# MLP up projection: high and low part of the left operand in one moving operand of 512 columns, and one weight sum formed by an accumulating load

## The chip, the cores and the metric

The kernel runs on one core of one Trainium2 chip. The metric is device time in microseconds of one execution. Lower is better. Before the change the median of three runs is 2542.24 us (2541.63 to 2547.61).

## What is computed

One layer of a streaming encoder: an input projection, stick-breaking attention beside a convolution module, a gated merge, and an MLP with squared ReLU. The change touches the first half of the MLP:

```
h = rmsnorm(x, g_pre_mlp[l])
f = jnp.square(jax.nn.relu(jnp.einsum('bsd,df->bsf', h, w_up[l])))
f = jnp.einsum('bsf,fd->bsd', f, w_down[l])
x = x + rmsnorm(f, g_post_mlp[l])
```

There are 512 tokens, 2048 channels (`D`) and 8192 hidden channels (`DFF`), all in float32.

## The kernel before

**Split products.** TensorE multiplies in a rounded 32-bit format. To keep float32 accuracy each operand is split into a high part (ScalarE copies and rounds, L74) and a low part (VectorE subtracts the high part, L75), and each product is three matmuls: high by high, weight high by activation low, weight low by activation high.

**The up stage.** The first 8 of 64 strips of 128 hidden channels are computed plainly. The other 56 go in 28 blocks of two strips, each block by a fast matrix scheme with seven products instead of eight. A product has a stationary operand that is a quarter of the block's weights or a sum of quarters, and a moving operand of 256 columns (half of the tokens, or a sum or difference of halves; held split in the tiles `h`, `s23` and `s4`). A product runs over `KC` = 8 slices of 128 channels, so it is 24 matmuls. The products of a block run in the order 3, 7, 1, 6, 5, 4, 2. They are called p3, p7 and so on below. The eight PSUM banks `bk` are used four by one block and four by the next. Within a block p5 adds onto the bank that p3 wrote, p4 onto the bank of p7, and p2 onto the bank of p1; p6 has a bank alone.

**The order around it** is written out by hand (`manual_schedule`). In step i, while product i runs, the engines get in this order: `grow` for product i+3 (VectorE adds another quarter of the weights to the running sum `tw`, L672), `prep` for product i+2 (ScalarE rounds 128x1024 weights into `whi_mlp`, VectorE forms `wlo_mlp`), `after_u` for product i-1 (reading its bank), and what earlier steps left for later (squared ReLU at L723 and L724; sums `sb` at L553 to L557 that are stored to memory by `spill`). Each queue is in order. There are three buffers for `whi_mlp`, so the rounding for product i+2 waits until product i-1 is done.

**The sums of weights.** p5 uses a sum of two quarters that comes ready from memory: SyncE's queue loads one quarter into `mlp_e` or `mlp_stat`, and GpSimd's queue loads the other on top with an accumulating DMA (`t1_next`, L664). p7, p6 and p4 use `tw`, one of four buffers loaded about three blocks ahead (`tw_next`, L655), to which `grow` adds one quarter before each of the three.

After the up stage comes the down projection with its own seven products a block (matmuls of 512 columns, L708). Its first loads read back what the up stage stored.

Of the kernel before, what the change touches and what calls it, by code (L numbers as in the profile page):

```python
# [10 lines left out]
AF = mybir.ActivationFunctionType  # L11
ALU = mybir.AluOpType
# [27 lines left out]
def block_kernel(ctx: ExitStack, tc: tile.TileContext, xT, w_qkgg, w_v, b_v, par, w_sb, w_cv, w_o, w_up, w_dn, g_post2, out):  # L40
# [13 lines left out]
    def st2(name, dt=F32R):  # L54
        t = wide(name, dt)
        return t[:, :T], t[:, T:]
# [434 lines left out]
    rstdy = cpool.tile([P, T], F32, tag="stat", bufs=4, name="rstdy")  # L491
    rms(rstdy, [ssy, sql], "rmsy")
    ss1 = cpool.tile([P, T], F32, tag="stat", bufs=4, name="ss1")
    X1, HG = [], []
    for e in range(KT):
        x1 = rt(f"x1_{e}")
        nc.sync.dma_start(x1, xT[e])
        X1.append(x1)
        HG.append(st2(f"h{e}"))
    with tc.manual_schedule(engines={mybir.EngineType.DVE}):  # L500
        for i in range(KT + 3):
            if i < KT:
# [61 lines left out]
    for i in range(PLAIN):  # L564
# [8 lines left out]
        spill(i, F, sb, 0)  # L573
        spill(i, F, sb, 1)
    UF = {}
    for k in range(KC):
        h1, h2 = X1[k], X1[k + KC]
        S.activation(h1, h1, AF.Identity, scale=col("g_pre2", k))
        S.activation(h2, h2, AF.Identity, scale=col("g_pre2", k + KC))
        V.tensor_tensor(out=h2[:, HT:], in0=h2[:, HT:], in1=h1[:, HT:], op=ALU.subtract)  # L580
        V.tensor_tensor(out=h1[:, HT:], in0=h1[:, :HT], in1=h1[:, HT:], op=ALU.subtract)
        V.scalar_tensor_tensor(out=h1[:, :HT], in0=h2[:, HT:], scalar=-1.0, in1=h1[:, :HT], op0=ALU.mult, op1=ALU.subtract)
        V.scalar_tensor_tensor(out=h2[:, :HT], in0=h2[:, :HT], scalar=-1.0, in1=h1[:, :HT], op0=ALU.mult, op1=ALU.subtract)
        hi, lo = st2(f"s23_{k}")
        split(hi, lo, h1)
        UF["s2", k], UF["s3", k] = (hi[:, :HT], lo[:, :HT]), (hi[:, HT:], lo[:, HT:])
        if k % 2 == 0:
            pair = st2(f"s4_{k}")
        hi, lo = [x[:, (k % 2) * HT:(k % 2 + 1) * HT] for x in pair]
        split(hi, lo, h2[:, :HT])  # L590
        UF["s4", k] = (hi, lo)
        for name, kt, o in (("a11", k, 0), ("s1", k, HT), ("a12", k + KC, 0), ("a22", k + KC, HT)):
            UF[name, k] = tuple(x[:, o:o + HT] for x in HG[kt])

# [21 lines left out]
    def bank(b, p):  # L618

        o = {3: 0, 5: 0, 7: 1, 4: 1, 1: 2, 2: 2, 6: 3}[p]  # L620
        if b[0] == "u":
            return bank8[4 * (b[1] % 2) + o][:, :HT]
        o = (o - 2 * b[1] - b[2]) % 4
        return bank8[2 * o:2 * o + 2]

# [26 lines left out]
    def tw_next():  # L652
        b, m = STEPS[state["tw"]]
        TW[b, m] = TWB[state["tw"] % 4]
        nc.sync.dma_start(TW[b, m], w_src(b, m, 0, 1))  # L655
        state["tw"] += 1

    def t1_next(tile=None):
# [8 lines left out]
    def grow(u):  # L667

        b, _, m, p = u
        by = {7: "b22", 6: "b11", 4: "b21"}.get(p)  # L670
        if by:
            V.tensor_tensor(out=TW[b, m], in0=TW[b, m], in1=RAW[b, by, m], op=ALU.add)  # L672

    W = {}
# [17 lines left out]
    def product(u):  # L692
        b, part, m, p = u
        wh, wl = W.pop(u)
        bk = bank(b, p)
        if b[0] == "u":
            for k in range(KC):
                ah, al = UF[LEFT[p], k]
                cs = slice(k * P, (k + 1) * P)
                for n, (w, a) in enumerate(((wh, ah), (wh, al), (wl, ah))):  # L700
                    PE.matmul(bk, lhsT=w[:, cs], rhs=a, start=part == 1 and k == 0 and n == 0, stop=k == KC - 1 and n == 2, skip_group_check=True)  # L701
            return
        for k2, t in ((0, 0), (0, 1), (1, 0), (1, 1)) if (b, m, p) != (END, 3, 2) else ((0, 0), (1, 0), (0, 1), (1, 1)):
            k = 2 * m + k2
            ws, ts_ = slice(k2 * T, (k2 + 1) * T), slice(t * P, (t + 1) * P)
            ah, al = FORM[LEFT[p], k]
            for n, (a, w) in enumerate(((ah, wh), (ah, wl), (al, wh))):
                PE.matmul(bk[t], lhsT=a[:, ts_], rhs=w[:, ws], start=part == 1 and k == 0 and n == 0, stop=k == KC - 1 and n == 2, skip_group_check=True)  # L708
# [5 lines left out]
    def after_u(i, u):  # L714
        b, _, _, p = u
        bk = {x: bank(b, x) for x in (3, 7, 1, 6)}
        if p == 3:
            UT[b] = (rt(f"uz{b[1]}"), [rt(f"f{2 * b[1] + n}") for n in range(2)], [rt(f"sb{b[1]}_{n}") for n in range(2)])
        uz, F, sb = UT[b]
        U, Z = uz[:, :HT], uz[:, HT:]  # L720

        def relu(n, op):
            V.scalar_tensor_tensor(out=F[n], in0=F[n], scalar=0.0, in1=rstd2, op0=op, op1=ALU.mult)  # L723
            S.activation(F[n], F[n], AF.Square)  # L724

        if p == 7:
            S.activation(Z, bk[3], AF.Copy)
            V.scalar_tensor_tensor(out=Z, in0=Z, scalar=-1.0, in1=bk[7], op0=ALU.mult, op1=ALU.add)
        if p == 6:
            S.activation(U, bk[1], AF.Copy)  # L730
            V.tensor_tensor(out=U, in0=U, in1=bk[6], op=ALU.add)
        if p == 5:
            V.tensor_tensor(out=F[1][:, :HT], in0=U, in1=bk[3], op=ALU.add)
            V.tensor_tensor(out=F[1][:, HT:], in0=F[1][:, :HT], in1=Z, op=ALU.add)
            later.append((i + 1, lambda: relu(1, ALU.min)))
        if p == 4:
            V.tensor_tensor(out=F[0][:, HT:], in0=U, in1=bk[7], op=ALU.add)
        if p == 2:
            S.activation(F[0][:, :HT], bk[1], AF.Copy)
            relu(0, ALU.max)  # L740
            later.append((i + 1, lambda: spill(b[1], F, sb, 0)))
            later.append((i + 2, lambda: spill(b[1], F, sb, 1)))
# [129 lines left out]
    with tc.manual_schedule():  # L872
        for n in range(RB):
            load_next()
            tw_next()
        t1_next()
        tw_next()
        t1_next()
        for i in range(-AH, N + 3):
            for j in ((i + AH + 1,) if i > -AH else (0, 1)):  # L880
                if j < N:
                    grow(UN[j])
            if i + AH < N:
                u = UN[i + AH]
                b, part, m, p = u
                prep(u)

                while state["load"] < len(LOADS) and all(at[x] + (0 if x[3] in (7, 6, 4) else 1) <= i + AH + 1 for x in LOADS[state["load"] - RB][2]):
                    load_next()
                if p == 5 and state["t1"] < len(STEPS) - 2:  # L890
                    t1_next()
                if p == 4 and state["tw"] < len(STEPS):
                    tw_next()
            if 1 <= i <= N:
                (after_u if UN[i - 1][0][0] == "u" else after_d)(i, UN[i - 1])
                if UN[i - 1] in ((END, 1, 2, 6), (END, 1, 3, 6)):
                    t1_next(st2(f"t1_late{i}", F32))
            for job in [x for x in later if x[0] <= i]:
                later.remove(job)
                job[1]()  # L900
            if i == 0:
                for k in range(KC):
                    hi, lo = UF["s1", k]
                    split(hi, lo, X1[k + KC][:, HT:])
            if pend_split and pend_split[0][0] <= i:
                form_split(pend_split.pop(0)[1])
            while pend_load and pend_load[0][0] <= i and len(pend_split) < (5 if len(pend_load[0][2]) > 1 else len(STG)):
                _, c, job = pend_load.pop(0)
                big = wide(f"fraw{i}", F32) if len(job) > 1 else None
                for n, (step, k) in enumerate(job):  # L910
                    if big is None:
                        raw = STG[state["form"] % len(STG)]
                        state["form"] += 1
                    else:
                        raw = big[:, n * T:(n + 1) * T]
                    pend_split.append((max(i + WAIT, DOWN - 5), form_load(c, step, k, raw)))
            if 0 <= i < N:
                u = UN[i]
                product(u)
                b, part, m, p = u  # L920
                if b[0] == "d" and b[2] == NE - 1 and b[1] < NK - 1:
                    if part == 1 and p == 6:
                        pend_load += [(i + LAG, b[1] + 1, ((step, k),)) for k in (2 * m, 2 * m + 1) for step in (1, 2)]
                    if part == 2 and p == 2:
                        pend_load += [(i + LAG, b[1] + 1, (job,)) for job in ((4, m), (3, 2 * m), (3, 2 * m + 1))]
# [46 lines left out]
```

## Time and profile before

| | |
|---|---|
| median of 3 runs | 2542.24 us |
| the profiled execution, its time and its span | 2542.73 us, 2541.0 us |
| TensorE matmul busy | 2487.4 us, 98% of the span |
| VectorE busy | 1740.4 us, 68% |
| ScalarE busy | 1066.9 us, 42% |
| chain that ended last | TensorE 94%, VectorE 3%, ScalarE 1%, L701 (the up products) 22% |
| DMA | 391.98 MB, mean 154 GB/s |

The busy share says which engine was occupied, the chain which engine the end waited for. Here both name TensorE over the whole program. Whether a stage stays so after a change to it can't be read from these averages; it needs the stage's own rows.

### The profile page before, as it was taken

The numbers are of one execution on the slowest core, as the hardware profiler recorded it, in microseconds if no ns is written. First come the engines' busy times: TensorE is split into PE (matmuls) and PEld (weight loads), VectorE is DVE, ScalarE is ACT, GpSimd is POOL, SyncE is SP. The second block draws the span as 40 slices with busy tenths as digits, with TensorE's granted clock in tenths as the row PEclk, the third lists the DMA queues.
The fourth block names the chain that finished last, engine by engine and source line by source line (L and its number), as shares of the span: only waits on it lengthen the run. The fifth ranks groups of instructions, "written<-read, shape, count | busy, mean of one in ns | idle before, by whom it ended". The sixth has DMA issues, their size and how long they took to land.

```text
span 2541.0 us, 34021 instructions
## 1 busy us (share of the span) xinstructions
PE 2487.4 (98%) x13312; PEld 2159.0 (85%) x13312; DVE 1740.4 (68%) x2304; ACT 1066.9 (42%) x1456; POOL 107.0 (4%) x128
## 2 busy tenths in 40 slices
PE   9999999999999999999899999999999999999995
PEld 7888888888888888887779999999998888888783
DVE  6355549999443334332778888878888787888877
ACT  5244443222342223232464444444456554545442
POOL 0000000000000000000000100000001000111000
PEclk9999999999999999999899999999999999999997
DMA  5222222332243223233166667666678666777674
GB/s 202 97 77 76 75 76 91 99 100 92 99 133 124 93 98 99 94 131 100 58 218 193 208 203 208 201 201 193 208 239 254 194 209 200 241 207 232 188 229 129
DMA packets 151793, 391.98 MB, mean 154 GB/s; under 512 B 16976, under 2 KB 25296, under 8 KB 151632
## 3 DMA queue, kind: packets, MB, share of 16 engines
q1 hardware_dynamic: 133776, 357.62, 41.5%
q0 software_dynamic: 17280, 31.46, 7.5%
q8 instruction: 104, 1.70, 0.3%
q10 hardware_dynamic: 576, 0.72, 0.1%
q14 instruction: 57, 0.47, 0.1%
HBM read 351.99 MB, written 37.75 MB: 153 GB/s over the span
## 4 chain that ended last, share of the span: by engine, by line
PE 94%; DVE 3%; ACT 1%; issue 1%; DMA 1%; SPq 0%; DVEq 0%; ACTq 0%
PE bk L701 22%; PE bk L708 21%; PE ps_in L87 9%; PE ps_in L88 9%; PE ps_in L89 9%; PE ps_o L87 2%; PE ps_o L88 2%; PE ps_o L89 2%; PE ps_up L88 1%; PE ps_up L89 1%; PE psv L87 1%; PE psv L89 1%; PE ps_up L87 1%; PE ps_sb L88 1%; PE psv L88 1%; PE ps_sb L89 1%
## 5 line engine op out<-in xcount | busy, mean ns | idle before, releaser
L708 PE MATMUL bk<-whi_mlp,ft 128*128 128x512 f32 x1792 | 554.8, 390 | 2.4 <-DVE ft L75 1.3
L708 PEld LDWEIGHTS bk<-whi_mlp,ft 128*128 128x128 f32 x1792 | 337.3, 188 | 74.6 <-DVE ft L75 2.1
L87 PE MATMUL ps_in<-x,whi_in 128*128 128x512 f32 x1024 | 399.7, 390 | 0.0
L88 PE MATMUL ps_in<-x,whi_in 128*128 128x512 f32 x1024 | 399.7, 390 | 0.0
L89 PE MATMUL ps_in<-x,wlo_in 128*128 128x512 f32 x1024 | 399.6, 390 | 0.0
L708 PE MATMUL bk<-wlo_mlp,ft 128*128 128x512 f32 x896 | 350.4, 391 | 9.1 <-DVE wlo_mlp L75 9.1
L701 PE MATMUL bk<-h,whi_mlp 128*128 128x256 f32 x1792 | 325.0, 283 | 0.0
L75 DVE TENSOR_TENSOR wlo_mlp<-tw,whi_mlp 128x1024 fp32r<-128x1024 f32 x180 | 220.2, 1223 | 135.9 <-ACT whi_mlp L74 135.8
L74 ACT ACTIVATE whi_in<-raw_in 128x1024 fp32r<-128x1024 f32 x128 | 135.8, 1061 | 402.2 <-PE ps_in L88 350.4
L74 ACT ACTIVATE whi_mlp<-tw 128x1024 fp32r<-128x1024 f32 x180 | 190.4, 1058 | 217.1 <-PE bk L701 91.7
L701 PEld LDWEIGHTS bk<-h,whi_mlp 128*128 128x128 f32 x1792 | 279.7, 192 | 0.0
L74 ACT ACTIVATE whi_mlp<-raw_mlp 128x1024 fp32r<-128x1024 f32 x180 | 190.4, 1058 | 202.2 <-PE bk L701 91.5
L75 DVE TENSOR_TENSOR wlo_mlp<-raw_mlp,whi_mlp 128x1024 fp32r<-128x1024 f32 x180 | 220.2, 1224 | 66.8 <-ACT whi_mlp L74 62.8
L701 PE MATMUL bk<-h,wlo_mlp 128*128 128x256 f32 x896 | 253.7, 283 | 0.0
L75 DVE TENSOR_TENSOR wlo_in<-raw_in,whi_in 128x1024 fp32r<-128x1024 f32 x128 | 156.6, 1223 | 134.1 <-ACT whi_in L74 134.0
L701 PE MATMUL bk<-s,whi_mlp 128*128 128x256 f32 x1344 | 244.3, 283 | 0.0
L89 PEld LDWEIGHTS ps_in<-x,wlo_in 128*128 128x128 f32 x1024 | 192.4, 188 | 39.3
L87 PEld LDWEIGHTS ps_in<-x,whi_in 128*128 128x128 f32 x1024 | 192.4, 188 | 39.3
L88 PEld LDWEIGHTS ps_in<-x,whi_in 128*128 128x128 f32 x1024 | 192.4, 188 | 38.9
L672 DVE TENSOR_TENSOR tw<-tw,raw_mlp 128x1024 f32<-128x1024 f32 x180 | 219.4, 1219 | 0.5
L701 PEld LDWEIGHTS bk<-s,whi_mlp 128*128 128x128 f32 x1344 | 209.8, 192 | 0.1
L708 PEld LDWEIGHTS bk<-wlo_mlp,ft 128*128 128x128 f32 x896 | 168.8, 188 | 46.3 <-DVE wlo_mlp L75 11.5
(292 smaller groups left out, 3790.4 us busy)
## 6 DMA issues: line engine op xcount, KB each, us to landing
raw_in<-w_qkgg SPq DMA_DIRECT2D x128, 512.0 KB, 3.4
raw_mlp<-w_dn SPq DMA_DIRECT2D x100, 512.0 KB, 4.1
raw_mlp<-w_up SPq DMA_DIRECT2D x84, 512.0 KB, 6.9
mlp_e<-dF SPq DMA_DIRECT2D x78, 256.0 KB, 4.0
raw_o<-w_o SPq DMA_DIRECT2D x32, 512.0 KB, 3.5
dF<-sb SPq DMA_DIRECT2D x64, 256.0 KB, 2.9
tw<-w_dn SPq DMA_DIRECT2D x32, 512.0 KB, 6.0
tw<-w_up SPq DMA_DIRECT2D x28, 512.0 KB, 6.6
```

What stands on the lines that cost most here:

```text
L74: S.activation(hi, src, AF.Copy)
L75: V.tensor_tensor(out=lo, in0=src, in1=f32(hi), op=ALU.subtract)
L87: PE.matmul(ps, lhsT=wh, rhs=xh, start=start, stop=False)
L88: PE.matmul(ps, lhsT=wh, rhs=xl, start=False, stop=False)
L89: PE.matmul(ps, lhsT=wl, rhs=xh, start=False, stop=stop)
L672: V.tensor_tensor(out=TW[b, m], in0=TW[b, m], in1=RAW[b, by, m], op=ALU.add)
L701: PE.matmul(bk, lhsT=w[:, cs], rhs=a, start=part == 1 and k == 0 and n == 0, stop=k == KC - 1 and n == 2, skip_group_check=True)
L708: PE.matmul(bk[t], lhsT=a[:, ts_], rhs=w[:, ws], start=part == 1 and k == 0 and n == 0, stop=k == KC - 1 and n == 2, skip_group_check=True)
```

## The change

Each product of the up stage takes the high and the low part of its activations in one matmul: the moving operand is the pair [high | low], 512 columns, against the high weights, into all 512 columns of the bank; a second matmul of 256 columns adds low weights by high activations to the right half. So a product is 16 matmuls instead of 24, and its result is the sum of the bank's two halves. `after_u` has to add these halves: `plus` is two additions, one after the other, where there was one. Also, the sum for p7 is formed by an accumulating load on GpSimd's queue behind the load of `tw`; `grow` for p7 is gone from VectorE.

```diff
+        HT2.append(wide(f"h{e}"))
+        HG.append((HT2[-1][:, :T], HT2[-1][:, T:]))
...
+    def both(t, o):
+        return t.rearrange("p (h n) -> p h n", h=2)[:, :, o:o + HT]
...
-            return bank8[4 * (b[1] % 2) + o][:, :HT]
+            return bank8[4 * (b[1] % 2) + o]
...
         nc.sync.dma_start(TW[b, m], w_src(b, m, 0, 1))
+        if b[0] == "u":
+            nc.gpsimd.dma_start(TW[b, m], w_src(b, m, 1, 1), accum_op=ALU.add)
...
-        if by:
+        if by and (b[0], p) != ("u", 7):
...
-                ah, al = UF[LEFT[p], k]
+                a = UF[LEFT[p], k]
                 cs = slice(k * P, (k + 1) * P)
-                for n, (w, a) in enumerate(((wh, ah), (wh, al), (wl, ah))):
-                    PE.matmul(bk, lhsT=w[:, cs], rhs=a, ...)
+                PE.matmul(bk, lhsT=wh[:, cs], rhs=a, ...)
+                PE.matmul(bk[:, HT:], lhsT=wl[:, cs], rhs=a[:, 0], ...)
...
+        def plus(dst, a, x, sign=ALU.add):
+            V.tensor_tensor(out=dst, in0=a, in1=bk[x][:, :HT], op=sign)
+            V.tensor_tensor(out=dst, in0=dst, in1=bk[x][:, HT:], op=sign)
+
         if p == 7:
-            S.activation(Z, bk[3], AF.Copy)
-            V.scalar_tensor_tensor(out=Z, in0=Z, scalar=-1.0, in1=bk[7], op0=ALU.mult, op1=ALU.add)
+            S.activation(Z, bk[7][:, :HT], AF.Copy)
+            V.tensor_tensor(out=Z, in0=Z, in1=bk[7][:, HT:], op=ALU.add)
+            plus(Z, Z, 3, ALU.subtract)
         if p == 6:
-            S.activation(U, bk[1], AF.Copy)
-            V.tensor_tensor(out=U, in0=U, in1=bk[6], op=ALU.add)
+            S.activation(U, bk[1][:, :HT], AF.Copy)
+            V.tensor_tensor(out=U, in0=U, in1=bk[1][:, HT:], op=ALU.add)
+            plus(U, U, 6)
         if p == 5:
-            V.tensor_tensor(out=F[1][:, :HT], in0=U, in1=bk[3], op=ALU.add)
+            plus(F[1][:, :HT], U, 3)
...
         if p == 4:
-            V.tensor_tensor(out=F[0][:, HT:], in0=U, in1=bk[7], op=ALU.add)
+            plus(F[0][:, HT:], U, 7)
         if p == 2:
-            S.activation(F[0][:, :HT], bk[1], AF.Copy)
+            S.activation(F[0][:, :HT], bk[1][:, :HT], AF.Copy)
+            V.tensor_tensor(out=F[0][:, :HT], in0=F[0][:, :HT], in1=bk[1][:, HT:], op=ALU.add)
             relu(0, ALU.max)
```

TensorE's queue at the end of p6 and the start of p5 of a block, before (`s` and `h` are split activations; in brackets the semaphores that a row waits for, named by the engine that raises them):

```order
L701 MATMUL bk_9432<-s_6_9412,wlo_mlp_9993 128x256
L701 MATMUL bk_9432<-s_7_9424,whi_mlp_9992 128x256 x2
L701 MATMUL bk_9432<-s_7_9424,wlo_mlp_9993 128x256
L701 MATMUL bk_9429<-h_8447,whi_mlp_10028 128x256 [waits Activation_49]
L701 MATMUL bk_9429<-h_8447,whi_mlp_10028 128x256
L701 MATMUL bk_9429<-h_8447,wlo_mlp_10029 128x256 [waits DVE_49]
```

and now:

```order
L709 MATMUL bk_9432<-s_6_9412,wlo_mlp_10266 128x256
L708 MATMUL bk_9432<-s_7_9424,whi_mlp_10265 128x512
L709 MATMUL bk_9432<-s_7_9424,wlo_mlp_10266 128x256
L708 MATMUL bk_9429<-h_8447,whi_mlp_10293 128x512 [waits DVE_49,Activation_49]
L709 MATMUL bk_9429<-h_8447,wlo_mlp_10294 128x256
```

The first matmul of p5 waited for ScalarE alone and now waits for VectorE too: for the last row of VectorE that reads this bank.

VectorE's queue of the same block from the `grow` for p4 on, before (`bk_9430` is the bank of p7):

```order
L672 TENSOR_TENSOR tw_9445<-tw_9445,raw_mlp_9866 128x1024 [waits DMAHW7_49,DVE_49]
L75 TENSOR_TENSOR wlo_mlp_10029<-mlp_e_9437,whi_mlp_10028 128x512 [waits DMASW4_49,PE_49,Activation_49]
L75 TENSOR_TENSOR wlo_mlp_10029<-mlp_e_9438,whi_mlp_10028 128x512 [waits DMASW5_49,Activation_49]
L728 SCALAR_TENSOR_TENSOR uz_9996<-uz_9996,bk_9430 128x256 [waits Activation_49]
L556 SCALAR_TENSOR_TENSOR sb_1_9763<-sb_1_9763,f_9760 128x256 [waits DVE_49]
```

and now (`bk_9429` is the bank of p3 and p5):

```order
L680 TENSOR_TENSOR tw_9443<-tw_9443,raw_mlp_10167 128x1024 [waits DMAHW3_49,DVE_49]
L75 TENSOR_TENSOR wlo_mlp_10294<-mlp_e_9437,whi_mlp_10293 128x512 [waits DMASW6_49,PE_49,Activation_49]
L75 TENSOR_TENSOR wlo_mlp_10294<-mlp_e_9438,whi_mlp_10293 128x512 [waits DMASW7_49,Activation_49]
L741 TENSOR_TENSOR uz_10269<-uz_10269,bk_9430 128x256 [waits Activation_49]
L736 TENSOR_TENSOR uz_10269<-uz_10269,bk_9429 128x256 [waits DVE_49]
L737 TENSOR_TENSOR uz_10269<-uz_10269,bk_9429 128x256 [waits DVE_49]
L557 SCALAR_TENSOR_TENSOR sb_1_10085<-sb_1_10085,f_10082 128x256
```

One row became three, each waiting for the row ahead of it, and the last two read the bank that p5 writes next. Before, ScalarE's copy (L727) had emptied that bank.

GpSimd's queue at the start of the up stage, before (`mlp_e` and `mlp_stat` hold the sums for p5):

```order
L664 DMA mlp_e_9437<-w_up 128x512 [waits DMAHW2_49,DMAHW6_49,DMAHW0_49,Activation_49]
L664 DMA mlp_e_9438<-w_up 128x512 [waits DMAHW4_49,DMAHW1_49,Activation_49]
L664 DMA mlp_stat_9441<-w_up 128x512 [waits DMAHW3_49,PE_49]
L664 DMA mlp_stat_9442<-w_up 128x512 [waits DMAHW4_49]
L664 DMA mlp_e_9437<-w_up 128x512 [waits DMAHW2_49]
```

and now:

```order
L663 DMA tw_9443<-w_up 128x1024 [waits DMAHW3_49,DVE_49,PE_49]
L663 DMA tw_9444<-w_up 128x1024 [waits DMAHW1_49,DVE_49]
L663 DMA tw_9445<-w_up 128x1024 [waits DMAHW3_49,PE_49]
L672 DMA mlp_e_9437<-w_up 128x512 [waits DMAHW2_49,DMAHW6_49,DMAHW0_49,Activation_49]
L672 DMA mlp_e_9438<-w_up 128x512 [waits DMAHW4_49,DMAHW1_49,Activation_49]
```

Three loads of 512 KB stand ahead of the first sum for p5; in later blocks one stands between the pairs.

## Rows read from the trace of the kernel before

**Rows 1.** Busy time in the up stage: us, each engine's busy time (instructions), clock, DMA.

```profile
1325.00:1889.48 564.48, 564.48 (x4706) 564.48 (x4705) 457.67 (x625) 265.28 (x373) 51.13 (x59) 1.00 0.69 205
```

**Rows 2.** Timeline of PE just ahead of the up stage: start, us; 512 columns.

```profile
1323.64 0.39 PE L87 MATMUL ps_up<-h,whi_up 128*128 128x512 f32 x1
...
1324.78 0.39 PE L89 MATMUL ps_up<-h,wlo_up 128*128 128x512 f32 x1
```

**Rows 3.** Timeline of PE: the first matmuls of p5 in one block.

```profile
1598.60 0.40 PE L701 MATMUL bk<-h,whi_mlp 128*128 128x256 f32 x2
```

**Rows 4.** Timeline of DVE from there: start, us; in brackets idle time and releaser.

```profile
1603.79 0.41 DVE L733 TENSOR_TENSOR f<-uz,bk 128x256 f32<-128x256 f32 x1
1604.24 0.42 DVE L734 TENSOR_TENSOR f<-f,uz 128x256 f32<-128x256 f32 x1
1605.58 1.22 DVE L75 TENSOR_TENSOR wlo_mlp<-tw,whi_mlp 128x1024 fp32r<-128x1024 f32 x1 [0.91 <-ACT whi_mlp L74]
1606.72 0.41 DVE L737 TENSOR_TENSOR f<-uz,bk 128x256 f32<-128x256 f32 x1
1607.05 0.68 DVE L723 SCALAR_TENSOR_TENSOR f<-f,rstd 128x512 f32<-128x512 f32 x1
...
1609.38 1.23 DVE L75 TENSOR_TENSOR wlo_mlp<-raw_mlp,whi_mlp 128x1024 fp32r<-128x1024 f32 x1 [0.51 <-ACT whi_mlp L74]
1610.52 0.68 DVE L723 SCALAR_TENSOR_TENSOR f<-f,rstd 128x512 f32<-128x512 f32 x1
1612.86 1.22 DVE L75 TENSOR_TENSOR wlo_mlp<-tw,whi_mlp 128x1024 fp32r<-128x1024 f32 x1 [1.65 <-ACT whi_mlp L74]
...
1614.67 1.22 DVE L672 TENSOR_TENSOR tw<-tw,raw_mlp 128x1024 f32<-128x1024 f32 x1
1615.81 1.28 DVE L75 TENSOR_TENSOR wlo_mlp<-mlp_e,whi_mlp 128x512 fp32r<-128x512 f32 x2
1617.01 0.41 DVE L728 SCALAR_TENSOR_TENSOR uz<-uz,bk 128x256 f32<-128x256 f32 x1
```

**Rows 5.** Timeline of ACT in the same stretch.

```profile
1604.48 1.06 ACT L74 ACTIVATE whi_mlp<-tw 128x1024 fp32r<-128x1024 f32 x1 [1.87 <-PE bk L701]
1607.77 0.63 ACT L724 ACTIVATE f<-f 128x512 f32<-128x512 f32 x1 [2.22 <-DVE f L723]
...
1611.24 0.63 ACT L724 ACTIVATE f<-f 128x512 f32<-128x512 f32 x1 [1.63 <-DVE f L723]
```

**Rows 6.** Timeline of DVE, then of PE, at a pause in the down projection.

```profile
1903.10 0.68 DVE L75 TENSOR_TENSOR ft<-fraw,ft 128x512 fp32r<-128x512 f32 x1
1903.84 0.73 PE L708 MATMUL bk<-whi_mlp,ft 128*128 128x512 f32 x2 [1.25 <-DVE ft L75]
1904.41 0.39 PE L708 MATMUL bk<-wlo_mlp,ft 128*128 128x512 f32 x1
```

**Rows 7.** Timeline of DVE in the last block of the up stage and behind it.

```profile
1879.09 0.41 DVE L728 SCALAR_TENSOR_TENSOR uz<-uz,bk 128x256 f32<-128x256 f32 x1
...
1888.07 1.23 DVE L75 TENSOR_TENSOR wlo_mlp<-tw,whi_mlp 128x1024 fp32r<-128x1024 f32 x1 [0.25 <-ACT whi_mlp L74]
...
1893.02 0.68 DVE L723 SCALAR_TENSOR_TENSOR f<-f,rstd 128x512 f32<-128x512 f32 x1
```

**Rows 8.** DMA by queue: packets, MB, share of 16 engines; q0 is the accumulating one.

```profile
q1 hardware_dynamic: 133776, 357.62, 41.5%
q0 software_dynamic: 17280, 31.46, 7.5%
```

**Rows 9.** Busy time just ahead of the up stage, columns as in the first group.

```profile
1316.00:1320.00 4.00, 4.00 (x19) 3.32 (x18) 0.48 (x1) 0.41 (x1) 0.00 (x0) 1.00 1.02 384
```

**Rows 10.** DMA issues: queue, count, KB, us to landing (median).

```profile
raw_mlp<-w_up SPq DMA_DIRECT2D x84, 512.0 KB, 6.9
mlp_e<-w_up POOLq DMA_DIRECT2D x28, 256.0 KB, 7.9
```

**Rows 11.** Timeline of SP's queue in the block of the fourth group.

```profile
1601.07 9.89 SPq L649 DMA_DIRECT2D raw_mlp<-w_up  x3
```

More of the change, by code (lines that the diff above doesn't have):

```diff
@@ L493, in block_kernel @@
     ss1 = cpool.tile([P, T], F32, tag="stat", bufs=4, name="ss1")
-    X1, HG = [], []
+    X1, HG, HT2 = [], [], []
     for e in range(KT):
@@ L498, in block_kernel @@
         X1.append(x1)
-        HG.append(st2(f"h{e}"))
+        HT2.append(wide(f"h{e}"))
+        HG.append((HT2[-1][:, :T], HT2[-1][:, T:]))
     with tc.manual_schedule(engines={mybir.EngineType.DVE}):
@@ L583, in block_kernel @@
         V.scalar_tensor_tensor(out=h2[:, :HT], in0=h2[:, :HT], scalar=-1.0, in1=h1[:, :HT], op0=ALU.mult, op1=ALU.subtract)
-        hi, lo = st2(f"s23_{k}")
-        split(hi, lo, h1)
-        UF["s2", k], UF["s3", k] = (hi[:, :HT], lo[:, :HT]), (hi[:, HT:], lo[:, HT:])
+        hi = wide(f"s23_{k}")
+        split(hi[:, :T], hi[:, T:], h1)
+        UF["s2", k], UF["s3", k] = both(hi, 0), both(hi, HT)
         if k % 2 == 0:
[L588 to L591, printed above, removed]
+            pair = wide(f"s4_{k}")
+        o = (k % 2) * HT
+        split(pair[:, o:o + HT], pair[:, T + o:T + o + HT], h2[:, :HT])
+        UF["s4", k] = both(pair, o)
         for name, kt, o in (("a11", k, 0), ("s1", k, HT), ("a12", k + KC, 0), ("a22", k + KC, HT)):
-            UF[name, k] = tuple(x[:, o:o + HT] for x in HG[kt])
+            UF[name, k] = both(HT2[kt], o)
     BLK_U = [("u", q) for q in range(PLAIN, NQ)]
@@ L697, in product @@
             for k in range(KC):
-                ah, al = UF[LEFT[p], k]
+                a = UF[LEFT[p], k]
                 cs = slice(k * P, (k + 1) * P)
-                for n, (w, a) in enumerate(((wh, ah), (wh, al), (wl, ah))):
-                    PE.matmul(bk, lhsT=w[:, cs], rhs=a, start=part == 1 and k == 0 and n == 0, stop=k == KC - 1 and n == 2, skip_group_check=True)
+                PE.matmul(bk, lhsT=wh[:, cs], rhs=a, start=part == 1 and k == 0, stop=k == KC - 1, skip_group_check=True)
+                PE.matmul(bk[:, HT:], lhsT=wl[:, cs], rhs=a[:, 0], start=False, stop=k == KC - 1, skip_group_check=True)
             return
@@ L902, in block_kernel @@
                 for k in range(KC):
-                    hi, lo = UF["s1", k]
-                    split(hi, lo, X1[k + KC][:, HT:])
+                    split(HG[k][0][:, HT:], HG[k][1][:, HT:], X1[k + KC][:, HT:])
             if pend_split and pend_split[0][0] <= i:
```

## The prediction

> **What bounds the kernel now.** I read the busy time of the up stage first [rows 1]: TensorE is busy in all of its 564.48 us, VectorE in 457.67. The view of waits has no wait of TensorE in this stretch. The 28 blocks have 28 x 7 x 24 = 4704 matmuls, so one takes 564.48 / 4704 = 0.120 us, a product 24 x 0.120 = 2.88 us and a block 20.16 us. Now the stage ends when TensorE has issued its matmuls.
>
> TensorE's busy share tells nothing of how close the others are behind it. So next I followed one block through the queues, from the start of p5 at 1598.60 [rows 3]. ScalarE begins to round the weights of the next p7 when p4, two products later, no longer needs its buffer (1604.48 [rows 5]). From there one thing hangs on the other [rows 4, 5]: VectorE's low part at 1605.58, the read of p4's bank at 1606.72 (L737), the scaling at 1607.05 (L723). ScalarE's queue stands until that scaling is done and squares at 1607.77 (L724); right behind it comes the rounding for p1, so its low part starts at 1609.38. Then the scaling of the other half at 1610.52, its square at 1611.24, the rounding for p6 and its low part at 1612.86, `grow` for p4 at 1614.67, two halves of p5's low part from 1615.81, and at 1617.01 the read of p7's bank (L728), which ends at 1617.42. VectorE's three waits in it (0.91, 0.51, 1.65 us) are all for ScalarE, which waited for VectorE (2.22 and 1.63 us). This is a second chain: 18.82 us from the start of p5 to the end of that read in the next block. The next p5 starts at 1598.60 + 20.16 = 1618.76 and doesn't need this read at all: p5 writes p3's bank, emptied by a ScalarE copy; the read of p7's bank is needed by p4, a product later. So the chain has some 4 us to spare, and TensorE sees nothing of it.
>
> **The change, part by part.**
>
> TensorE. Matmuls of 512 columns follow each other in (1324.78 - 1323.64) / 5 = 0.228 us [rows 2], those of 256 in 0.120. A product becomes 8 x (0.228 + 0.120) = 2.784 us: 0.096 less, 0.67 us a block, 18.8 us over 28 blocks, if nothing makes TensorE wait. A moving operand in two pieces (two runs of 256 columns, 512 apart) is not in the trace; I take it at the price of one run.
>
> The Trainium skill (TensorE: Matmul & The Clock Gate, section "Back-to-back issue gap") gives a matmul N / 2.4 + 2.5 ns, so only 2.5 ns are saved with each matmul left out. The rows show 0.120 and 0.228 where it gives 0.109 and 0.216. By it a product would save 8 x 2.5 ns = 0.02 us, and the stage 3.9 us in place of 18.8.
>
> VectorE. Seven additions of 256 columns come in per block (0.41 us each) and one `grow` (1.22 us) goes. In busy time that is 7 x 0.41 - 1.22 = +1.7 us on 457.67 / 28 = 16.3, about 18.0 of 19.5 us: it would still fit. Where they stand decides. The `grow` for p7 stands ahead of a low part that waits for ScalarE anyway (0.91 us idle at 1605.58): taking it out shortens the chain by nothing. Of the new additions four lie on the chain: one ahead of the scaling at 1607.05, one ahead of that at 1610.52, two behind the first read at 1617.01. Each waits for the row ahead of it, and two such rows start 1604.24 - 1603.79 = 0.45 us apart [rows 4]. Four are 1.80 us. The lower bound is 0.34 each, the distance between rows that don't wait for each other (1607.05 - 1606.72): 1.34 us. The upper bound I put at 0.52 each (the row's own 0.41 and the 0.11 by which 0.45 is above 0.34). I take 0.45, since the order shows the waits.
>
> The wait that is added. The last two of these additions read p3's bank, and p5's first matmul now waits for the last of them. The other additions are off the chain: those for p6's bank must be read before p2, two products later, and p5's come behind the low part for the next p3.
>
> So p5 can't start again sooner than 18.82 us, less the two shorter products in the chain (0.19), plus 1.80, plus 0.06 us from VectorE's end to TensorE's start (1903.10 + 0.68 = 1903.78, 1903.84), plus what a restart costs: two matmuls took 1904.41 - 1903.84 = 0.57 us where two paced ones take 0.46, so 0.11 [rows 6]. Together 20.60 us. TensorE needs 7 x 2.784 = 19.49 us: it waits 1.1 us in each block, at p5, and a block takes 0.44 us more than the 20.16 now. Behind the waiting matmul stand p5, p4 and p2; for them wait the rounding of the next weights and with it the same chain, so the wait comes back in every block and does not fade.
>
> The Trainium skill (PSUM — Partial Sum Buffer, section "PSUM bank collisions raise a hardware error") has two engines never in one bank at once, so p5 could not start on columns already read. No row here shows that; the order shows the one wait for the whole bank.
>
> The sum. The first block meets no such wait, and its p5 starts four products of 0.096 sooner: -0.4 us. From the first p5 to the last are 27 blocks: 27 x 0.44 = +11.9 us. Then the handover to the down projection, where the chain runs on through VectorE and ScalarE to a pause of TensorE at 1903.84. In the last block the read at 1879.09 ends 1.34 us ahead of p5 (1598.60 + 14 x 20.16 = 1880.84), after the change 0.06: 1.28 us later. Up to the scaling at 1893.02 five more additions at 0.45 come in, 2.25 us, and about 0.4 us goes in the waits for ScalarE (0.25 at 1888.07 [rows 7], and the addition fits partly behind it): +3.1 us.
>
> The accumulating load. By queue [rows 8], 31.46 MB take 7.5% of 2541.0 us on 16 engines, 6.1 us per MB; the plain queue 2.9. One of 512 KB is 3.2 us of all engines, 0.16 of a block on top of a share of 0.69 [rows 1]; it fits. In steady state its sum is needed three blocks later. Ahead of the first block it may not be free: three such loads stand ahead of the first sum for p5 on GpSimd's queue when the DMA engines are full already (1.02 [rows 9]) and GpSimd's loads take 7.9 us to land without them [rows 10]. Bounds: 0, and about 5 us once (9.6 us of work, less what the emptier time before takes up and some slack). I take 1.5.
>
> Together -0.4 + 11.9 + 3.1 + 1.5 = +16.1 us on the profiled execution's 2542.73; its time is 0.5 us above the median. That gives 2558.
>
> **The rivals.**
>
> TensorE stays the bound. If the chain does not close (if ScalarE or VectorE reaches the new rows sooner than the order lets me see), p5 never waits and the gain is 18.8 us less 0 to 5: 2523.5. For it speaks that TensorE has no wait now; against it, that the chain would have to be 1.1 us shorter a block, more than the 0.46 us that the lower price of four additions gives. The point from which it decides is a chain of 19.49 us. By the Trainium skill's price of a matmul (same page and section) this case's gain would be 3.9 us, 2538.5; the pace at both widths speaks against that price, and I give it 0.01 of this case's chance.
>
> The two cancel. With four additions at 0.34, the block takes 20.14 us, -0.5 us over 27; with -0.4 and +2.6 at the handover the time is about 2544: no change.
>
> A transfer late in each block. The quarter `b21` is asked for at 1601.07 [rows 11] and added at 1614.67, 13.6 us later; it lands in 6.9 us [rows 10]. Beside an accumulating load twice as long it may take 3 to 6 us more, which still fits. If it took over 13.6 us, each us of it would cost 28: 2586 at one us. The distance speaks against it.
>
> **How the numbers follow.** Chances: the wait at p5 as worked out 0.60; the two cancel 0.18; TensorE stays the bound 0.13; a late transfer 0.09. About 0.3% (7.6 us) is what a measurement of this kernel can tell from no change. The first and the last are slower; of the second I give a small part to either side: faster 0.13, same 0.19, slower 0.68. The range runs from 2542, the cancelling case at the low price with no loss at the start, to 2571: 2558 plus 3.5 (the start at its bound) plus 7.6 (27 x 4 x 0.07, additions at 0.52) and some of the late transfers. Left out are TensorE as the bound and most of the late transfers, 2 in 10.
>
> **What would show it.** The profile after should show 3136 matmuls of 512 and 256 columns 0.228 and 0.120 us apart; TensorE idle about 1.1 us ahead of p5's first matmul in each block but the first, released by the second subtraction on p3's bank; blocks of 20.6 us; VectorE's three rows on these banks 0.45 us apart. I am wrong if TensorE has no idle time there, if the wait is on another product, if blocks take under 20.2 us, or if the DMA is what a wait names.

## The result, and the profile after

The changed kernel takes 2567.86 us (median of four runs, 2564.95 to 2570.11) against 2543.57 us for the kernel before in the same session (2541.63 to 2547.61). The ratio is 1.0089 (95% interval 1.0074 to 1.0104): slower by 0.9%. The forecast was 2558, range 2542 to 2571. The profiled executions stand 2564.95 to 2542.73, +22.2 us where +16.1 was worked out.

The page of the kernel after: busy time by engine, the accumulating queue, the chain that ended last.

```profile
PE 2478.2 (97%) x11744; PEld 2072.3 (81%) x11744; DVE 1786.8 (70%) x2472; ACT 1063.4 (41%) x1456; POOL 131.6 (5%) x156
...
q0 software_dynamic: 21312, 46.15, 10.9%
...
PE 86%; DVE 8%; issue 2%; ACT 2%; DMA 1%; ACTq 0%; POOL 0%; DVEq 0%; SPq 0%; POOLq 0%
```

The busy shares have hardly moved, but the chain has: TensorE's share of it fell from 94% to 86%, and VectorE's rose from 3% to 8%. The up stage by itself (columns as in [rows 1]):

```profile
1323.80:1907.20 583.40, 555.41 (x3137) 480.48 (x3135) 501.49 (x788) 260.68 (x371) 74.60 (x85) 1.00 0.80 223
```

It is 583.40 us long where it was 564.48, and TensorE is idle in 28 us of it, which it never was before. The view of its waits, in that stage and then from the second block on, names one place (us in total, times, longest):

```profile
PE bk L708 <- DVE uz L737: 28.0, 28, 4.5
...
PE bk L708 <- DVE uz L737: 23.5, 27, 1.0
```

L708 is the 512-column matmul, and L737 the second half of `plus`, here the second subtraction on p3's bank. The wait stands in every block, once, at p5: 4.5 us in the first, 23.5 / 27 = 0.87 us in the others. VectorE in one block (start, us, line; in brackets idle time and releaser), to set against [rows 4]:

```profile
1617.75 0.41 DVE L736 TENSOR_TENSOR f<-uz,bk 128x256 f32<-128x256 f32 x1
1618.20 0.42 DVE L737 TENSOR_TENSOR f<-f,bk 128x256 f32<-128x256 f32 x1
1618.54 0.69 DVE L731 SCALAR_TENSOR_TENSOR f<-f,rstd 128x512 f32<-128x512 f32 x1
...
1620.88 1.23 DVE L75 TENSOR_TENSOR wlo_mlp<-raw_mlp,whi_mlp 128x1024 fp32r<-128x1024 f32 x1 [0.52 <-ACT whi_mlp L74]
1622.02 0.41 DVE L755 TENSOR_TENSOR f<-f,bk 128x256 f32<-128x256 f32 x1
1622.47 0.69 DVE L731 SCALAR_TENSOR_TENSOR f<-f,rstd 128x512 f32<-128x512 f32 x1
1624.81 1.23 DVE L75 TENSOR_TENSOR wlo_mlp<-tw,whi_mlp 128x1024 fp32r<-128x1024 f32 x1 [1.65 <-ACT whi_mlp L74]
...
1627.75 1.29 DVE L75 TENSOR_TENSOR wlo_mlp<-mlp_e,whi_mlp 128x512 fp32r<-128x512 f32 x2
1628.96 0.41 DVE L741 TENSOR_TENSOR uz<-uz,bk 128x256 f32<-128x256 f32 x1
1629.41 0.42 DVE L736 TENSOR_TENSOR uz<-uz,bk 128x256 f32<-128x256 f32 x1
1629.86 0.42 DVE L737 TENSOR_TENSOR uz<-uz,bk 128x256 f32<-128x256 f32 x1
...
1637.23 1.23 DVE L75 TENSOR_TENSOR wlo_mlp<-tw,whi_mlp 128x1024 fp32r<-128x1024 f32 x1 [0.26 <-ACT whi_mlp L74]
```

ScalarE's two squares (L732) wait for the two scalings (L731), as in [rows 5]:

```profile
1619.26 0.63 ACT L732 ACTIVATE f<-f 128x512 f32<-128x512 f32 x1 [2.68 <-DVE f L731]
...
1623.19 0.63 ACT L732 ACTIVATE f<-f 128x512 f32<-128x512 f32 x1 [2.08 <-DVE f L731]
```

And TensorE at the end of p6 and the start of p5:

```profile
1627.80 0.40 PE L708 MATMUL bk<-s,whi_mlp 128*128 128x512 f32 x1
...
1629.21 0.40 PE L708 MATMUL bk<-s,whi_mlp 128*128 128x512 f32 x1
1629.44 0.28 PE L709 MATMUL bk<-s,wlo_mlp 128*128 128x256 f32 x1
1630.43 0.47 PE L708 MATMUL bk<-h,whi_mlp 128*128 128x512 f32 x1 [0.71 <-DVE uz L737]
...
1630.86 0.39 PE L708 MATMUL bk<-h,whi_mlp 128*128 128x512 f32 x1
...
1632.24 0.39 PE L708 MATMUL bk<-h,whi_mlp 128*128 128x512 f32 x1
```

The three rows on the banks start 0.45 us apart, and the last ends at 1630.28, 0.15 us ahead of p5. The second subtraction is the last link of the second chain, and TensorE the one that waits. From the first matmul of each p3 (L708) one gets the length of each block: from the second, at 1349.68, to the 27th, at 1866.13, 25 blocks take 516.45 us, 20.66 each. They run in a cycle of 20.57, 20.62 and 20.78.

Where the 22.2 us stand, by the starts of p5. Of before these are 1336.52 (1598.60 - 13 x 20.16) in the first block and 1880.84 in the last; of after, 1339.71 and 1898.92 (rows below).

| stretch | predicted | measured |
|---|---|---|
| up to p5 of the first block | +1.1 | +3.2 |
| 27 blocks to p5 of the last | +11.9 | +14.9 |
| handover and the rest | +3.1 | +4.1 |

**The first block.** GpSimd issues its loads (L663 adds onto `tw`, L672 onto the sums for p5):

```profile
1309.11 1.01 POOL L663 DMA_DIRECT2D tw<-w_up  x1 [1306.68 <-DVE sb L557]
...
1321.61 0.86 POOL L663 DMA_DIRECT2D tw<-w_up  x1 [1.65 <-DMA tw<-w_up]
...
1324.61 0.88 POOL L672 DMA_DIRECT2D mlp_e<-w_up  x1 [2.15 <-DMA mlp_e<-w_up]
1328.70 0.86 POOL L672 DMA_DIRECT2D mlp_e<-w_up  x1 [3.20 <-DMA tw<-w_up]
```

ScalarE then stands until these sums have landed:

```profile
1334.51 0.63 ACT L74 ACTIVATE whi_mlp<-mlp_e 128x512 fp32r<-128x512 f32 x1 [5.71 <-DMA mlp_e<-w_up]
1336.96 0.63 ACT L74 ACTIVATE whi_mlp<-mlp_e 128x512 fp32r<-128x512 f32 x1 [1.82 <-DMA mlp_e<-w_up]
```

TensorE's p5 in the first block and in the last, and the pause in the down projection that [rows 6] shows of before:

```profile
1339.71 0.76 PE L708 MATMUL bk<-h,whi_mlp 128*128 128x512 f32 x1 [4.47 <-DVE uz L737]
...
1898.92 0.47 PE L708 MATMUL bk<-h,whi_mlp 128*128 128x512 f32 x1 [0.97 <-DVE uz L737]
...
1926.65 0.73 PE L716 MATMUL bk<-whi_mlp,ft 128*128 128x512 f32 x2 [1.25 <-DVE ft L75]
```

The windows around the first p5 (the last three columns: granted clock, DMA share, GB/s):

```profile
1336.00:1340.00 4.00, 0.29 (x1) 0.32 (x2) 2.31 (x5) 3.04 (x5) 0.88 (x1) 0.93 1.07 290
1340.00:1344.00 4.00, 4.00 (x16) 3.38 (x16) 3.01 (x5) 0.03 (x1) 0.00 (x0) 0.64 1.09 258
```

The sums for p5 come late while the DMA engines are full (1.07 and 1.09), p5 starts 4.4 us later after the stage's start than before (1339.71 - 1323.79 against 1336.52 - 1325.00), and behind that idle time the granted clock falls to 0.64 over four microseconds, partly the 1.2 GHz level. This p5 takes 4.32 us where later ones take 2.85 to 2.89, 1.5 more. That makes about 5.9 us at the start. The stage itself began 1.2 us earlier in this execution; in the other traces below it begins anywhere from 1323.9 to 1329.2, so I put that down to scatter.

### The profile page after: what moved, and what is told of

It is laid out like the page before. It is cut to its first block, busy times and chain, and to the rows that moved or that the text cites. A ratio compares the mean times of both kernels' runs of the same rounds, so it can differ in the third digit from the quotient of the medians.

```text
span 2563.1 us, 31060 instructions
## 1 busy us (share of the span) xinstructions
PE 2478.2 (97%) x11744; PEld 2072.3 (81%) x11744; DVE 1786.8 (70%) x2472; ACT 1063.4 (41%) x1456; POOL 131.6 (5%) x156
## 4 chain that ended last, share of the span: by engine, by line
PE 86%; DVE 8%; issue 2%; ACT 2%; DMA 1%; ACTq 0%; POOL 0%; DVEq 0%; SPq 0%; POOLq 0%
PE bk L716 22%; PE bk L708 10%; PE ps_in L88 9%; PE ps_in L87 9%; PE ps_in L89 9%; PE bk L709 5%; PE ps_o L88 2%; PE ps_o L87 2%; PE ps_o L89 2%; DVE wlo_mlp L75 2%; DVE tw L680 1%; ACT whi_mlp L74 1%; PE psv L87 1%; PE ps_sb L88 1%; PE psv L89 1%
## 5 line engine op out<-in xcount | busy, mean ns | idle before, releaser
L708 PE MATMUL bk<-h,whi_mlp 128*128 128x512 f32 x896 | 318.8, 398 | 28.0 <-DVE uz L737 28.0
L709 PE MATMUL bk<-h,wlo_mlp 128*128 128x256 f32 x896 | 251.8, 281 | 0.0
L708 PE MATMUL bk<-s,whi_mlp 128*128 128x512 f32 x672 | 237.1, 394 | 0.0
L708 PEld LDWEIGHTS bk<-h,whi_mlp 128*128 128x128 f32 x896 | 168.5, 188 | 73.7 <-issue 30.0
L709 PE MATMUL bk<-s,wlo_mlp 128*128 128x256 f32 x672 | 188.3, 280 | 0.0
L680 DVE TENSOR_TENSOR tw<-tw,raw_mlp 128x1024 f32<-128x1024 f32 x152 | 185.5, 1220 | 0.5
```

The source lines that it names most:

```text
L708: PE.matmul(bk, lhsT=wh[:, cs], rhs=a, start=part == 1 and k == 0, stop=k == KC - 1, skip_group_check=True)
L709: PE.matmul(bk[:, HT:], lhsT=wl[:, cs], rhs=a[:, 0], start=False, stop=k == KC - 1, skip_group_check=True)
```

## The experiments

Theory 1 is the prediction's: a chain of VectorE and ScalarE closes on p5 through p3's bank, and what counts is the length of that chain, not how much work the engines have. Theory 2: VectorE and the DMA engines have too much to do in the stage (VectorE's work is 501.49 us instead of 457.67, the DMA share 0.80 instead of 0.69), and the place of a row matters little. Lengths of blocks are taken as above, over blocks 2 to 26; waits are those of TensorE.

**1. The squares a step later.** Nothing is taken out. ScalarE gets each square behind the next rounding and not ahead of it, so that a rounding no longer waits for VectorE's scaling.

```diff
-        def relu(n, op):
+        def relu(n, op, now):
             V.scalar_tensor_tensor(out=F[n], in0=F[n], scalar=0.0, in1=rstd2, op0=op, op1=ALU.mult)
-            S.activation(F[n], F[n], AF.Square)
+            later.append((now + 1, lambda: S.activation(F[n], F[n], AF.Square)))
...
-            later.append((i + 1, lambda: relu(1, ALU.min)))
+            later.append((i + 1, lambda: relu(1, ALU.min, i + 1)))
...
-            relu(0, ALU.max)
+            relu(0, ALU.max, i)
```

> The changed kernel, with the two squares of the squared ReLU given to ScalarE one step later, behind the rounding for the next product in place of ahead of it. Work, transfers and matmuls stay the same. Theory 1 (the chain: VectorE's additions wait for ScalarE's rounding, which stands behind a square that waits for VectorE): the chain is cut, TensorE has no wait at p5 from the second block on, blocks take 19.4 to 19.8 us in place of 20.66, so 23 to 34 us less over 27 blocks and 1 to 4 less at the handover: 2527 to 2541. The cost of about 6 us in the first block stays. Theory 2 (the amount: seven more additions on VectorE, or the added transfers, slow the stage wherever they stand): nothing changes, 2565.

Measured: 2533.36 us (2528.35 to 2542.89, nine runs), 0.9959 of before (0.9944 to 0.9973); the profiled execution 2528.35. The waits of the up stage, then ScalarE in one block:

```profile
PE bk L708 <- DVE uz L737: 4.7, 1, 4.7
```

```profile
1602.54 1.06 ACT L74 ACTIVATE whi_mlp<-raw_mlp 128x1024 fp32r<-128x1024 f32 x1 [1.71 <-PE bk L708]
...
1603.77 0.62 ACT L732 ACTIVATE f<-f 128x512 f32<-128x512 f32 x1
1605.36 1.06 ACT L74 ACTIVATE whi_mlp<-tw 128x1024 fp32r<-128x1024 f32 x1 [0.97 <-PE bk L708]
```

Each rounding now starts when TensorE has done with its buffer; none stands behind a square that waits for VectorE. The 27 waits at p5 are gone; the one in the first block is left. Blocks take 19.41 us. VectorE has as much to do as in the changed kernel (503.19 us in the stage) and the DMA engines move the same loads (a share of 0.85), so Theory 2 falls here.

**2. The same edit on the kernel before.** A control: do the later squares gain anything where TensorE doesn't wait?

> The kernel before, with the squares one step later as its only edit: a control for the two runs with the squares moved. Theory 1 (the chain): TensorE never waits in the up stage before, so blocks stay at 20.16 us and only the handover to the down projection may gain up to 3 us: 2539 to 2543. If the move were a gain by itself, the time would fall by 10 us or more.

Measured: 2542.08 us (2540.99 to 2543.62, ten runs), 0.9987 of before (0.9978 to 0.9996), and no wait in the stage. It gives 0.1%, so the gain of experiment 1 is the wait that goes, and the shorter products that then show.

**3. `grow` for p7 back on VectorE.** The accumulating load onto `tw` is gone, the rest of the change stays.

```diff
-        if b[0] == "u":
-            nc.gpsimd.dma_start(TW[b, m], w_src(b, m, 1, 1), accum_op=ALU.add)
...
-        if by and (b[0], p) != ("u", 7):
+        if by:
```

> The changed kernel, with the weight sum for p7 back on VectorE and no added accumulating load. Theory 1 (the chain): the sum's row stands ahead of p7's low part where the additions have used up the idle time, so the chain gets 0.7 to 0.9 us longer, blocks of 21.3 to 21.5 us, 27 x 0.75 = 20 us slower, and the 6 us at the first block are gone: about 2579. Theory 2 in its form of transfers (the added accumulating load costs the stage its time): without it the time falls to 2545 to 2550. Theory 2 in its form of VectorE's work: 27 x 1.2 = 32 us slower, about 2591.

Measured: 2582.12 us (2581.60 to 2582.31, four runs), 1.0142 of before (1.0128 to 1.0155). The first block takes 19.63 us and has no wait; the others take 21.39, which is 0.73 more than in the changed kernel. So the load buys 27 x 0.73 = 19.8 us and costs some 6 at the start, in all about 14: the medians of the two lie 14.3 us apart. Theory 2 in its form of transfers had this kernel faster than the changed one; it is slower. In before VectorE had 0.91 us idle at that place [rows 4], and taking a row out there would have shortened nothing. In the changed kernel 0.26 us is left of it (the row at 1637.23): the added rows have used it up, and so has the room that `grow` left.

**4. Both edits.**

> Both edits: squares one step later, and the weight sum for p7 on VectorE with no added accumulating load. Theory 1 (the chain): once the chain is cut VectorE has room for the sum, blocks of 19.4 us on TensorE's own pace (19.8 if its slower pace stays), no cost in the first block: 2520 to 2526, at the slower pace up to 2535, faster than both kernels. Theory 2 (the amount): VectorE has more to do than in the changed kernel, so 2565 or more.

Measured: 2536.19 us (2525.80 to 2536.75, five runs), 0.9961 of before (0.9947 to 0.9974); the profiled execution 2525.80, blocks 19.41, the first 19.63, no wait. The grow that cost 0.73 us a block in experiment 3 costs nothing where the chain doesn't close.

**5. One addition less, on the chain or off it.** Two kernels leave out one of the seven new additions each, and with it part of the sum: the first the low half of p2 (L755), which stands ahead of the second scaling; the second one half of p6's bank.

```diff
-            V.tensor_tensor(out=F[0][:, :HT], in0=F[0][:, :HT], in1=bk[1][:, HT:], op=ALU.add)
```

```diff
-            plus(U, U, 6)
+            V.tensor_tensor(out=U, in0=U, in1=bk[6][:, :HT], op=ALU.add)
```

> The changed kernel without one addition a block: the high half alone of p2's bank goes on (the low half is left out of the result). This addition stands on the chain, ahead of the second scaling. Theory 1 (the chain): blocks 0.45 us shorter than the 20.66 of the changed kernel, 20.2, and 12 us less in all: 2553. Theory 2 (the amount of work on VectorE): 0.33 us of VectorE's time less in each of 28 blocks, 9 us: 2556. Alone it doesn't tell the two apart; with the next run it does.

> The changed kernel without another addition a block: the right half of p6's bank is left out of the result. This addition stands off the chain, ahead of idle time of VectorE at p7's low part. Theory 1 (the chain): nothing changes, blocks of 20.66 us, 2565. Theory 2 (the amount): as in the run with the other addition out, 9 us less, 2556.

Measured in one run each: 2558.60 and 2571.61 us. The waits of the first one from the second block on:

```profile
PE bk L708 <- DVE uz L737: 10.4, 27, 0.5
```

That is 0.39 us a block instead of 0.87, and blocks of 20.21 instead of 20.66: the one row on the chain is worth 0.45 us, the distance at which it stands from the next. The second has blocks of 20.66, as if nothing had been left out. Both rows are 0.41 us of VectorE's time. That is the second proof against Theory 2. (The time of the second kernel is above the changed kernel's in its one run. Of the 6.7 us to that kernel's profiled execution, 2.6 stand in the first block, 28.5 us instead of 25.9, and 2.3 are a later start of the stage.)

**6. p3's bank read a product earlier.** The bank that p5 waits for is read right behind p3; p7's is then subtracted from.

```diff
+        if p == 3:
+            S.activation(Z, bk[3][:, :HT], AF.Copy)
+            V.tensor_tensor(out=Z, in0=Z, in1=bk[3][:, HT:], op=ALU.add)
         if p == 7:
-            S.activation(Z, bk[7][:, :HT], AF.Copy)
+            V.scalar_tensor_tensor(out=Z, in0=Z, scalar=-1.0, in1=bk[7][:, :HT], op0=ALU.mult, op1=ALU.add)
             V.tensor_tensor(out=Z, in0=Z, in1=bk[7][:, HT:], op=ALU.add)
-            plus(Z, Z, 3, ALU.subtract)
```

> The changed kernel with p3's bank read one product earlier, right after p3, into the same tile; p7's bank is then combined with it. As many rows on each engine as before the edit. Theory 1 (the chain): p5 no longer waits for a read, but the additions stay in the chain ahead of the low parts of the weights, and TensorE meets it a little later, at p6 and p4, with 0.2 and 0.5 us a block: blocks of about 20.1 us, 15 us less, 2550. If the wait for the bank were all, blocks would fall to 19.4 and the time to 2531. Theory 2 (the amount): 2565.

Measured: 2550.46 us (2548.40 to 2552.39, ten runs), 1.0023 of before (1.0014 to 1.0032). Blocks take 20.16 us, and the wait stands elsewhere (L709 is the 256-column matmul with the low weights):

```profile
PE bk L709 <- DVE wlo_mlp L75: 4.8, 20, 0.7
```

p5 is free, and half a microsecond a block is won; the first block takes 22.0 us instead of 25.9. But the chain through the squares still can't go round in the 19.41 us that TensorE would need: p4 and, less so, p6 now wait for their low weights (up to 3.32 and 3.03 us where an unhindered product takes 2.77). Removing the last link moves the wait; removing the link between the engines (experiment 1) removes it.

**7. The accumulating load alone, on the kernel before.**

```diff
+        if b[0] == "u":
+            nc.gpsimd.dma_start(TW[b, m], w_src(b, m, 1, 1), accum_op=ALU.add)
...
-        if by:
+        if by and (b[0], p) != ("u", 7):
```

> The kernel before with one part of the change alone: the weight sum for p7 by the accumulating load. Theory 1: TensorE's pace and the blocks stay at 20.16 us, the load costs in the first block alone, where the first sum for p5 comes late by some 4 to 6 us: 2546 to 2549 against 2542.7. If the added transfers cost in every block (theory 2 in that form), 0.3 us a block or more: 2552 or more.

Measured: 2549.76 us (2545.80 to 2553.15, ten runs), 1.0016 of before (1.0006 to 1.0025): 4 to 5 us. The first block takes 24.53 us instead of 20.15, and all others 20.16. ScalarE in the first block, and the windows around its p5:

```profile
1335.88 0.63 ACT L74 ACTIVATE whi_mlp<-mlp_e 128x512 fp32r<-128x512 f32 x1 [5.75 <-DMA mlp_e<-w_up]
```

```profile
1338.00:1342.00 4.00, 2.59 (x17) 2.59 (x18) 2.69 (x4) 3.07 (x5) 0.88 (x1) 0.87 1.08 262
1342.00:1346.00 4.00, 4.00 (x26) 4.00 (x26) 2.42 (x4) 1.06 (x1) 0.00 (x0) 0.70 1.09 276
```

It is the same picture as in the changed kernel, without the 512-column matmuls: a late sum for p5, then a clock of 0.70. So most of the start term comes with the load. The changed kernel adds to it, since its p5 also waits for the three reads behind the late sum: TensorE stands for 4.5 us there, and for 2.6 here. With the load kept and p3's bank read early (experiment 6) the first block was 3.9 us shorter.

**8. Why the times of one kernel lie 10 us apart.** The kernel of experiment 4 has runs from 2525.80 to 2536.75. It was run twice more as it is, for a profile of either kind, beside a version in which odd slices take their two matmuls in the other order (512, 256, 256, 512 columns, and so on).

```diff
-                PE.matmul(bk, lhsT=wh[:, cs], rhs=a, ...)
-                PE.matmul(bk[:, HT:], lhsT=wl[:, cs], rhs=a[:, 0], ...)
+                for n in (0, 1) if k % 2 == 0 else (1, 0):
+                    if n == 0:
+                        PE.matmul(bk, lhsT=wh[:, cs], rhs=a, ...)
+                    else:
+                        PE.matmul(bk[:, HT:], lhsT=wl[:, cs], rhs=a[:, 0], ...)
```

> The kernel with both edits once more, unchanged. Its profiled execution took 2525.8 us with products of 2.774 us from the first block's fifth on and 2.83 us before; four timed executions took 2535 to 2537. If the slower pace can last, 28 blocks of 7 x 0.057 us more are 11 us, which is that difference: then this profile shows 2.774 throughout at about 2526 or 2.83 throughout at about 2536, or a change of pace between and a time between. If the pace has nothing to do with it, a time near 2536 comes with products of 2.774 us and the difference stands elsewhere in the trace.

> A third look at the kernel with both edits, for the same question as the second: whether the pace of the products, 2.774 or 2.83 us, accounts for the time, 2526 or 2536.

> The same kernel with the two matmuls of every second slice in the other order, so that matmuls of 512 columns stand in pairs and those of 256 in pairs. The sum of columns and the number of matmuls are the same. If the slower pace comes from how a long and a short matmul alternate, the products take 2.78 us in all executions and the time is 2526 with little spread; if it comes from the state at a start or a restart alone, both paces show again, 2526 to 2537.

Measured: the two runs gave 2528.53 and 2540.15 us. TensorE in the first, then in the second, in the same stretch:

```profile
1611.67 0.39 PE L706 MATMUL bk<-h,whi_mlp 128*128 128x512 f32 x1
...
1613.05 0.39 PE L706 MATMUL bk<-h,whi_mlp 128*128 128x512 f32 x1
```

```profile
1611.82 0.40 PE L706 MATMUL bk<-h,whi_mlp 128*128 128x512 f32 x1
...
1613.23 0.40 PE L706 MATMUL bk<-h,whi_mlp 128*128 128x512 f32 x1
```

Four pairs of matmuls take 1.38 us in the one and 1.41 in the other. All products from the middle of the first block on have that pace, 2.774 us in the one and 2.82 to 2.83 in the other, and blocks take 19.41 and 19.79: over the stage that is 10.2 us of the 11.6 between them; 1.3 more is the later start of the stage.

In the alternating order all products from the sixth on take 2.787 us, and blocks 19.51. Its time is 2525.62 us (2523.97 to 2528.35, five runs), 0.9922 of before (0.9909 to 0.9936). It is the best version here, faster than both kernels.

## Why the prediction was right, and which terms were off

**The mechanism held at each step.** TensorE ran short by waiting for VectorE at p5, in each block, released by the second subtraction on p3's bank, as the text on p5 said. In two blocks of three it is 3.90 us from the start of p6 to that of p5, where a p6 takes 2.77 without the wait: 1.13 us. The restart makes p5 0.08 longer. Together that is 1.21 us, where 1.1 was worked out for both. Rows that wait for the row ahead of them stand 0.45 us apart; experiment 5 measures the price of one at 0.45. Blocks take 20.66 us against 20.60. Moving the link that closes the chain (experiment 1) takes the wait away with no work taken out.

**The shorter product.** 2.774 us where 2.784 was worked out, at the quicker of two paces. By the Trainium skill (TensorE: Matmul & The Clock Gate, section "Back-to-back issue gap") a matmul left out saves 2.5 ns, which would put a product at 2.86 us and a block at no less than 20.0. Experiment 1's blocks of 19.41 say otherwise: here the rows decide, 0.12 us for 256 columns and 0.23 for 512. The prediction took that price for one of a stream; the section gives it for a matmul by itself. Its figure for a stream of weight loads and matmuls, about 131 ns at 512 columns, doesn't fit these rows either.

**The term for the start was too small.** I took 1.5 us, with 5 as the bound. It is about 5.9: 4.4 of waiting and 1.5 of lower clock behind it. The prediction had the first block without the wait at p5; it has the longest one. I had the three loads ahead of the sums for p5 on GpSimd's queue, but priced them by the work of the DMA engines, less what an emptier time would take up. The queue stood between its loads, and the second of the pair was only issued at 1328.70. The first had waited 2.15 us for its plain load to land. The row of the second names a load onto `tw`, which this sum has no need of; its own plain load had landed at 1324.60 (the last mark of that transfer in the trace). What fits all thirteen traces is a limit: never more than three of GpSimd's loads are in flight, and 26 times, all around the first block, a load starts 0.25 to 0.31 us after the one three places ahead of it has landed. Here that is the second load onto `tw`, landed at 1328.44; in before the first sums for p5, with nothing in flight, went out at 1323.33 and 1324.03. So the three loads held the places that the sums needed. What sets the limit is not shown, and in three of the experiments' traces it was the second sum's own plain load that landed late (1329.45 to 1332.80).

And I had no term for the clock behind such a pause. Experiment 7 has 4.4 us of waiting and clock together with the load alone.

**The blocks** came to 27 x 0.50 = 13.4 us and not 11.9: from VectorE's end to p5 it is 0.15 us where [rows 6] gave 0.06, and in one block of three the products run at the slower pace; a restart of 0.08 instead of 0.11 takes a little back.

**The handover** came to 4.1 and not 3.1. At the pause [rows 6] it was 4.7, of which 0.6 came back later. VectorE's rows up to the last scaling hold 1.2 for the late read (1.28 predicted) and 2.27 for five additions (2.25 predicted). But I had 0.4 us vanish in waits for ScalarE, and instead ScalarE itself waited for the read back of a stored sum, which landed later (5.45 us of idle time, 1.61 at that place in before):

```profile
1908.37 0.63 ACT L74 ACTIVATE ft<-mlp_e 128x512 fp32r<-128x512 f32 x1 [5.45 <-DMA mlp_e<-dF]
```

```profile
1909.03 0.69 DVE L75 TENSOR_TENSOR ft<-mlp_e,ft 128x512 fp32r<-128x512 f32 x1 [1.23 <-ACT ft L74]
```

VectorE's 1.23 us there have no counterpart at that place in before. Together: 5.9 + 13.4 + 4.1, less the 1.2 by which the stage began earlier, are the 22.2 us measured.

**The rivals.** That TensorE stays the bound was forecast at 2523.5; it needed a chain of under 19.49 us, and the kernels that have it (experiments 1 and 4) reach 2528.35 and 2525.80 in their profiled executions (medians 2533.36 and 2536.19). The cancelling case needed additions at 0.34. A transfer late in each block did not come: behind the first block TensorE waits for the chain alone, and the waits of VectorE in the block shown are for ScalarE's roundings.

**Luck in the range.** The measured 2567.86 us lies 3 us inside the upper end of 2571. That end had 7.6 us for additions at 0.52, which measured 0.45, and some for late transfers, which did not come. What used this room was the start, beyond its bound of 5, and the blocks and the handover. That the range was wide enough for these is luck; the path and the price of the additions are not.

## What to carry to other kernels

A gain on the busiest engine is worth only the room up to the next chain that returns to it, and that chain is found by following one block through the queues of the other engines, not by their busy shares: a row of 0.41 us cost 0.45 us a block or nothing, by where it stood. Where two engines in order wait for each other in turn, look first for a row that nobody needs soon (here a square) standing ahead of one that the other engine waits for; one step later, it turned 0.9% slower into 0.4% faster. A load moved onto a queue in order should be checked at the first block by itself, where nothing has run ahead and one pause also costs clock.

## What the runs showed of the hardware that I had not expected

**Two paces of one instruction stream.** A pair of a 512-column and a 256-column matmul takes 347 ns or 353 ns (blocks of 56 pairs in 19.41 and 19.79 us), in the changed kernel both: the rows above have four pairs in 1.41 us from 1627.80 and four in 1.38 from 1630.86, at a granted clock of 1.00, on either side of one wait. In the changed kernel the pace changes at the waits and holds between them. In the kernel of experiment 4 it changed once, within p5 of the first block, with no wait in view, in two traces, and in the third it stayed the slower one for the whole stage, which makes 10 us. In the three traces with 256-column matmuls alone a product took 2.88 from the second block on. In the alternating order one pace shows, 2.787, in one trace, and five times lie within 4.4 us. What sets the pace stays open, and so does why the order of the two widths matters.

**Three loads in flight.** GpSimd's accumulating loads never overlap more than three deep in any trace here; the term for the start above has the times.

**What one pause costs.** In the first block TensorE stood for 4.5 us, and the following pairs were 0.64 us apart before they came back to 0.35 (granted clock 0.64 over those four microseconds). The pauses of 0.9 us in each later block left the clock alone (1.00 over the stage).
